# A transformer block on one Trainium2 core: the first FFN opened by token tile in a hand-written order, with the second half of x loaded behind four weight rows

## The chip, the cores and the metric

The kernel runs on one NeuronCore of a Trainium2 chip. The time is device microseconds of one execution. Three runs of the kernel before took 1849.17, 1852.2 and 1852.67 us; their median is 1852.2 us. The profiles come from single executions of their own; a profile's span runs from the first instruction to the last.

## The reference

One block of depth 1 over 256 tokens of width 2048, all in float32, with three parts in a row: a gated FFN (SwiGLU, inner width 5632), a mixer (differential attention beside a causal depthwise convolution), and a second FFN. Each part begins with an RMS norm, whose result is scaled and shifted by values that come from a conditioning vector `c`. The change concerns the first part alone:

```python
c_act = jax.nn.silu(c)
ada = jnp.einsum('bd,de->be', c_act, w_ada[l]) + b_ada[l]     # 9 x 2048 values
sh1, sc1, g1, ... = jnp.split(ada, N_MOD, axis=-1)
h = modulate(rms_norm(x, ffn1_norm[l]), sh1, sc1)             # h * (1 + sc1) + sh1
gu = jnp.einsum('bsd,df->bsf', h, w_gu); g, u = jnp.split(gu, 2, axis=-1)
x = x + FFN_RESIDUAL_WEIGHT * g1[:, None, :] * jnp.einsum('bsf,fd->bsd', jax.nn.silu(g) * u, w_down)
```

So before the first product with `w_gu` there must be: x and its root mean square for each token, the conditioning vector, and the scale and shift of the first 128 channels, which are dot products of `c_act` with rows of `w_ada`.

## The kernel before

**Tiles.** The 256 tokens are two tiles of 128 (t = 0, 1), the 2048 channels 16 tiles of 128 (k), the 11264 columns of `w_gu` 22 chunks of 512 (c). A weight row, here, is what one k brings to one chunk: 128 x 512 float32, 256 KB. Each float32 operand is split in two, a rounded part hi and a rest lo: ScalarE (ACT) casts hi, VectorE (DVE) subtracts to get lo. A product of one k, chunk and token tile is then three matmuls of 512 columns on TensorE (PE): ah x wh, ah x wl, al x wh (`mm3`, lines 316 to 318). A weight row so takes six matmuls for both token tiles, one split on ACT and one on DVE.

**Ada rows.** The modulation is computed on DVE. A row of 128 outputs is a 1 MB transfer and one multiply-and-sum over 2048 columns (`ada`, lines 181 and 182) against `c_bc`, the activated vector spread over all partitions by 16 PE transposes at the very start. Rows come in pairs, scale and shift of one k. The first two are brought and summed in halves (`first_modulation`, line 239), so that k = 0 is ready soon. `ada_next` counts the rows that have been traced, from 2 on.

**Opening.** h of a k can only be formed when its two ada rows are in. So the first chunks are not computed over a whole quarter of the channels (4 k), but over as many k as are ready: `EXT` gives the number for each chunk (1 for the first eight, 2 for four, 3 for three, then 4). `LOADS` says which chunks come in one transfer. Chunks with one k come through `w_first`, the others through `w_tile`. Their sums are kept in SBUF as `parts`. What is left of the quarter is made up later: the chunks in `AGAIN` are opened once more for their remaining k, and the result is added to the part by two DVE additions (line 538); the chunks in `EARLY` get their remaining k together with the next quarters in one accumulation.

**Order before.** x is loaded in two transfers right behind the constants. Both tiles' squares are summed, both are normed and transposed (`begin_both`, line 399 and 401), then `first_modulation` runs with the first weight row between its third and its fourth half, and `tile` (lines 387 to 389) forms hi and lo of h for both token tiles at once. In the loop at line 501 a chunk is loaded and split `AHEAD` = 3 steps before its products, ada rows follow the loads by `FIRST_ADA` and then by `DUE` (pairs of weight rows and ada rows that are due by then, with a straight line between), and `stage_a` makes the products of a chunk for both token tiles and copies them to the part (line 469).

**What sets the order.** The framework schedules the instructions of every engine ahead of time by its own cost figures; each engine then runs its own list strictly in order. `issue_after` adds an edge that puts instructions of an engine behind a given one on that engine; it is used for the transfers, all of which are on SP's queue. Buffers: 28 blocks of 4 KB per partition (`blk`), 4 raw buffers of 8 KB (shared by ada rows and full weight tiles), 4 hi and 4 lo buffers of two weight rows each, 6 accumulators in PSUM (`acc`) and 2 for transposes (`tp`).

Of the kernel before, what the change touches and what calls it, by code (L numbers as in the profile page):

```python
# [16 lines left out]
F32 = mybir.dt.float32  # L17
F32R = mybir.dt.float32r
# [9 lines left out]
NT = 2  # L28
# [9 lines left out]
DVE_COLS = 2  # L38
SOONER = 150
AHEAD = 3  # L40
EXT = (1,) * 8 + (2,) * 4 + (3,) * 3
LOADS = [(0,), (1,), (2, 3), (4, 5), (6, 7)] + [(c,) for c in range(8, NCH)]
FIRST_ADA = (0, 0, 1, 1, 1, 1, 1, 0, 1, 1, 1, 1)
AGAIN = [4, 5, 6]
EARLY = [[3, 8, 9], [4, 5, 6], [7, 10, 11], [12, 13, 14]]
EARLY_3 = [13, 14]

DUE = ((19, 8), (55, 16), (107, 24), (150, 32))


TAPS = (6, 8, 7, 6, 6, 6, 8, 6, 6, 6)
# [24 lines left out]
def block_kernel(ctx: ExitStack, tc: tile.TileContext, x_in, pos_in, w_ada, small, w_gu1, w_dn1,  # L76
# [41 lines left out]
    for t in range(NT):  # L118
        nc.sync.dma_start(out=xall[:, t, :], in_=x_in[t * P:(t + 1) * P, :])
# [75 lines left out]

    def ada_due(rows):

        r0, j0 = 0, 2
        for r, j in DUE:
# [26 lines left out]
            mods[base, k] = (G, a[:, j % 8 + 1:j % 8 + 2])  # L226
        return mods[base, k]

    def first_modulation(between):

        ada_cols[0] = const.tile([P, 8], F32, name="ada0")
        p0 = _COLS["bada"][0]
        a = sm([P, 4], "adah")
        for i in range(2):
            for h in range(2):
                between(2 * i + h)
                wa = blk([P, 1024])
                hs = slice(1024 * h, 1024 * h + 1024)
                nc.sync.dma_start(out=wa, in_=w_ada[i, :, hs])
                nc.vector.tensor_tensor_reduce(out=wa, in0=wa, in1=c_bc[:, hs], scale=1.0, scalar=0.0, op0=ALU.mult,  # L240
                                               op1=ALU.add, accum_out=a[:, 2 * i + h:2 * i + h + 1])
            nc.vector.scalar_tensor_tensor(out=ada_cols[0][:, i:i + 1], in0=a[:, 2 * i:2 * i + 1],
                                           scalar=cst[:, p0 + i:p0 + i + 1], in1=a[:, 2 * i + 1:2 * i + 2],
                                           op0=ALU.add, op1=ALU.add)
            if i == 0:
                nc.vector.scalar_tensor_tensor(out=scales[:, 0:1], in0=ada_cols[0][:, 0:1], scalar=1.0,
                                               in1=col("n1")[:, 0:1], op0=ALU.add, op1=ALU.mult)
        mods[0, 0] = (scales[:, 0:1], ada_cols[0][:, 1:2])
# [50 lines left out]
                views[k0 + h + j] = (hi[:, j, :], lo[:, j, :])  # L299
        return lambda j: views[j]  # L300

    def w_first(cs):
# [4 lines left out]
        hi = whp.tile([P, 2, 512], F32R, tag="whi", name=nm("whi"))  # L307
        lo = wlp.tile([P, 2, 512], F32R, tag="wlo", name=nm("wlo"))
        nc.scalar.copy(out=hi[:, :n, :], in_=raw[:, :n, :])
        nc.vector.tensor_sub(out=lo[:, :n, :], in0=raw[:, :n, :], in1=hi[:, :n, :].bitcast(F32))  # L310
        return [lambda j, i=i: (hi[:, i, :], lo[:, i, :]) for i in range(n)]

    def mm3(acc, a, w, start, stop):
        ah, al = a
        wh, wl = w
        nc.tensor.matmul(acc, ah, wh, start=start, stop=False)  # L316
        nc.tensor.matmul(acc, ah, wl, start=False, stop=False)  # L317
        return nc.tensor.matmul(acc, al, wh, start=False, stop=stop)  # L318

# [26 lines left out]
    class Norm:  # L346
# [41 lines left out]
            nc.vector.tensor_scalar(out=hf, in0=src, scalar1=G, scalar2=SH, op0=ALU.mult, op1=ALU.add)  # L388
            self.last = nc.vector.tensor_sub(out=self.hl[k // 4][:, k % 4, ts], in0=hf, in1=hi.bitcast(F32))  # L389

        def begin_both(self):
# [3 lines left out]
            for t in range(NT):  # L395
                self.done.add((0, t))
                self.rstd(t)
                xn = tmp([P, 512])
                nc.scalar.activation(out=xn, in_=x[0][:, t, :], func=AF.Identity, scale=self.r[t])
                for j in range(4):  # L400
                    nc.tensor.transpose(tps[j // 2][:, j % 2, t * P:(t + 1) * P], xn[:, j * P:(j + 1) * P], ident)
            return [tps[j // 2][:, j % 2, :] for j in range(4)]
# [39 lines left out]
    def ffn(st, w_gu, w_dn, gate_base, ada_a, ada_b, nxt, again, early, early_3):  # L442
# [36 lines left out]
        ext = [4] * NCH  # L479
        if not st.done:  # L480

            raws, begun = st.begin_both(), [0]
            ws = {}

            def load(i):
                cs = LOADS[i]
                if ext[cs[0]] == 1:
                    ws.update(zip(cs, w_first(cs)))
                else:
                    ws[cs[0]] = w_tile(w_gu[cs[0], 0], False, (0, ext[cs[0]]), ext[cs[0]] < 4)  # L490
# [3 lines left out]
            def begin_ready():
                while begun[0] < 4 and base + 2 * begun[0] + 2 <= ada_next[0]:
                    st.tile(raws[begun[0]], tmp([P, S]), (begun[0], slice(0, S)))
                    begun[0] += 1

            first_modulation(lambda n: load(0) if n == 3 else None)
            begin_ready()  # L500
            for i in range(len(LOADS) + AHEAD):
                if i < len(LOADS):
                    if i:
                        load(i)
                    with tc.issue_after(w_dma[0].ins):
                        if i < len(FIRST_ADA):
                            ada_until(ada_next[0] + FIRST_ADA[i])
                            rows[0] += ext[LOADS[i][0]] * len(LOADS[i])
                        else:
                            ada_a_share(ext[LOADS[i][0]])  # L510
# [677 lines left out]
```

## Time and profile before

| what | value |
| --- | --- |
| median of three runs | 1852.2 us |
| the profiled execution | 1848.81 us |
| its span | 1847.0 us |
| PE busy | 1820.2 us, 99% of the span |
| DVE busy | 1442.0 us, 78% |
| ACT busy | 911.9 us, 49% |
| mean granted TensorE clock | 0.996 |
| first matmul on a weight row | 17.66 us |

PE, DVE, ACT and POOL are the compute engines, SP the queue that issues the transfers. In a listing by time, a row gives the start and the length in us, engine, line, operation, output<-input and a count of merged instructions, then in brackets the idle time of the engine before it and what ended it. In a list of groups, the columns are count, busy us, mean ns of one, and the idle time before them with its releasers. In a table of windows the columns are the stretch, its length, busy time and number of instructions of PE, of its weight loads, of DVE, ACT and POOL, then the granted PE clock, the share of the DMA engines in use and GB/s. Matmuls are pipelined: the start of one to the start of the next is the time that it takes, not the length shown.

### The profile page before, as it was taken

What the parts mean: (1) busy time and instruction counts of PE and PEld (TensorE: products, weight loads), DVE (VectorE), ACT (ScalarE), POOL (GpSimd) and SP (SyncE); (2) the same over time, 40 slices, a digit from 0 to 9 for tenths busy, and PEclk for the clock granted to TensorE, in tenths of its full rate; (3) what the DMA queues carried; (4) which work ended last, traced back from release to release, by engine and by line L of the source; (5) the groups of instructions that cost most, each with busy time, mean ns of one, the idle gap of its engine ahead of it and who ended that gap; (6) DMA issues with size and microseconds to landing.
All of it is one profiled execution on the core that took longest, in us unless ns stands there. A gap on an engine that the chain in (4) does not pass through costs nothing.

```text
span 1847.0 us, 21889 instructions
## 1 busy us (share of the span) xinstructions
PE 1820.2 (99%) x8247; PEld 1501.6 (81%) x8247; DVE 1442.0 (78%) x1922; ACT 911.9 (49%) x1378; POOL 26.5 (1%) x29
## 2 busy tenths in 40 slices
PE   6999999999999999999999999999999999999999
PEld 5788888888888887878888888888888888888887
DVE  7789969998888777899999668878877765544443
ACT  6553444444444433554777655664444444433332
POOL 0000000000000000000110000000000000000000
PEclk8999999999999999999999999999999999999999
DMA  9888968888899898765544458888777755565552
GB/s 381 348 316 307 342 254 316 333 308 338 323 346 350 335 357 329 284 228 205 182 160 138 172 216 306 333 328 318 280 279 273 276 191 194 183 211 211 200 210 80
DMA packets 72729, 495.91 MB, mean 268 GB/s; under 512 B 8192, under 2 KB 8624, under 8 KB 15152
## 3 DMA queue, kind: packets, MB, share of 16 engines
q1 hardware_dynamic: 72624, 494.53, 72.1%
q8 instruction: 64, 1.05, 0.2%
q14 instruction: 41, 0.34, 0.1%
HBM read 492.37 MB, written 2.12 MB: 268 GB/s over the span
## 4 chain that ended last, share of the span: by engine, by line
PE 93%; DVE 3%; ACT 1%; DMA 1%; issue 1%; POOL 0%; SPq 0%; POOLq 0%; DVEq 0%; ACTq 0%
PE acc L317 30%; PE acc L318 30%; PE acc L316 30%; DVE blk L772 1%; PE tp L589 1%; DVE wlo L297 1%; DMA blk<-in_w_gu_dram 1%; PE acc L864 1%; PE tp L378 1%; DMA blk<-in_w_ada_dram 1%; ACT whi L295 0%; PE acc L903 0%; DVE raw L182 0%; ACT blk L469 0%; PE tp L813 0%
## 5 line engine op out<-in xcount | busy, mean ns | idle before, releaser
L295 ACT CAST whi<-raw 128x1024 fp32r<-128x1024 f32 (+1 forms) x605 | 628.4, 1046 | 737.5 <-PE acc L318 613.6
L297 DVE TENSOR_TENSOR wlo<-raw,whi 128x1024 fp32r<-128x1024 f32 (+1 forms) x605 | 725.7, 1212 | 318.3 <-ACT whi L295 316.9
L316 PE MATMUL acc<-whi,blk 128*128 128x512 f32 x2448 | 957.0, 393 | 5.8 <-ACT blk L387 2.2
L317 PE MATMUL acc<-wlo,blk 128*128 128x512 f32 x2448 | 956.7, 391 | 4.6 <-DVE wlo L297 4.6
L318 PE MATMUL acc<-whi,blk 128*128 128x512 f32 x2448 | 956.1, 391 | 0.1
L316 PEld LDWEIGHTS acc<-whi,blk 128*128 128x128 f32 x2448 | 460.5, 188 | 102.0 <-ACT whi L295 2.8
L317 PEld LDWEIGHTS acc<-wlo,blk 128*128 128x128 f32 x2448 | 460.6, 188 | 101.1 <-DVE wlo L297 8.0
L318 PEld LDWEIGHTS acc<-whi,blk 128*128 128x128 f32 x2448 | 460.2, 188 | 97.1 <-DVE blk L389 0.9
L182 DVE CUSTOM_DVE_ANT_0 raw<-raw,c_bc 128x2048 f32<-128x2048 f32 x142 | 324.4, 2285 | 5.3 <-DMA raw<-in_w_ada_dram 4.8
L772 DVE SCALAR_TENSOR_TENSOR blk<-blk,cst,blk 128x255 f32<-128x255 f32 (+17 forms) x240 | 97.5, 463 | 0.5 <-ACT blk L770 0.5
L469 ACT COPY blk<-acc 128x512 f32<-128x512 f32 x88 | 49.8, 591 | 60.6 <-PE acc L318 58.8
L581 DVE TENSOR_TENSOR blk<-acc,blk 128x512 f32<-128x512 f32 x88 | 56.9, 683 | 0.3
L318 PE MATMUL acc<-blk,blk 128*128 128x512 f32 x112 | 43.7, 392 | 0.0
L316 PE MATMUL acc<-blk,blk 128*128 128x512 f32 x112 | 43.7, 393 | 0.0
L317 PE MATMUL acc<-blk,blk 128*128 128x512 f32 x112 | 43.7, 390 | 0.0
L297 DVE TENSOR_TENSOR blk<-raw,blk 128x1024 fp32r<-128x1024 f32 x28 | 33.7, 1220 | 1.8 <-ACT blk L295 1.8
L583 DVE TENSOR_TENSOR blk<-blk 128x256 f32<-128x256 f32 x88 | 33.4, 418 | 0.7 <-ACT blk L582 0.7
L582 ACT ACTIVATE blk<-blk 128x256 f32<-128x256 f32 x88 | 32.2, 411 | 0.8 <-DVE blk L581 0.8
L295 ACT CAST blk<-raw 128x1024 fp32r<-128x1024 f32 x28 | 28.8, 1049 | 6.6 <-DMA raw<-in_w_dn_dram 5.3
L335 DVE TENSOR_TENSOR blk<-tp,blk 128x512 fp32r<-128x512 f32 x44 | 30.0, 684 | 2.3 <-ACT blk L334 2.3
L344 ACT ACTIVATE tmp<-xall 128x512 f32<-128x512 f32 x22 | 13.8, 631 | 31.2 <-DVE xall L642 17.8
L334 ACT CAST blk<-tp 128x512 fp32r<-128x512 f32 x44 | 25.3, 580 | 2.4 <-PE tp L589 2.4
(149 smaller groups left out, 662.8 us busy)
## 6 DMA issues: line engine op xcount, KB each, us to landing
raw<-in_w_gu_dram SPq DMA_DIRECT2D x161, 1024.0 KB, 5.2
raw<-in_w_ada_dram SPq DMA_DIRECT2D x142, 1024.0 KB, 5.9
raw<-in_w_dn_dram SPq DMA_DIRECT2D x88, 1024.0 KB, 4.8
raw<-in_w_in_dram SPq DMA_DIRECT2D x40, 1024.0 KB, 4.8
raw<-in_w_out_dram SPq DMA_DIRECT2D x16, 1024.0 KB, 4.8
raw<-in_w_gu_dram SPq DMA_DIRECT2D x8, 768.0 KB, 5.2
blk<-in_w_gu_dram SPq DMA_DIRECT2D x10, 512.0 KB, 14.1
blk<-gate_line SPq DMA_DIRECT2D x6, 512.0 KB, 5.6
```

What stands on the lines that cost most here:

```text
L182: nc.vector.tensor_tensor_reduce(out=raw, in0=raw, in1=c_bc, scale=1.0, scalar=0.0, op0=ALU.mult, op1=ALU.add, accum_out=ada_cols[g][:, j ...
L295: nc.scalar.copy(out=hi[:, :m, :], in_=rw)
L297: nc.vector.tensor_sub(out=lo[:, :m, :], in0=rw, in1=hi[:, :m, :].bitcast(F32))
L316: nc.tensor.matmul(acc, ah, wh, start=start, stop=False)
L317: nc.tensor.matmul(acc, ah, wl, start=False, stop=False)
L318: return nc.tensor.matmul(acc, al, wh, start=False, stop=stop)
L335: nc.vector.tensor_sub(out=lo, in0=tp, in1=hi.bitcast(F32))
L469: last_part[0] = nc.scalar.copy(out=parts[c][:, t, :], in_=accs[t])
L581: nc.vector.tensor_add(out=p[:, t, :], in0=accs[t], in1=p[:, t, :])
L582: nc.scalar.activation(out=p[:, t, :256], in_=p[:, t, :256], func=AF.Silu)
L583: nc.vector.tensor_mul(out=p[:, t, 256:], in0=p[:, t, :256], in1=p[:, t, 256:])
L772: nc.vector.scalar_tensor_tensor(out=y[:, d:], in0=u, scalar=w, in1=y[:, d:], op0=ALU.mult, op1=ALU.add)
```

## The change

The opening is traced by token tile.

- x of tile 0 is loaded as before; x of tile 1 is loaded behind the transfers of loads 0 to 2 (weight rows of chunks 0 to 3, `X_BEHIND`).
- Tile 0 alone is squared, normed and transposed, and then comes `first_modulation`, with no weight row between its halves.
- Loads 0 to 4 (chunks 0 to 7, one k each) are all issued at once; the hi and lo of loads 3 and 4 lie in blocks instead of the shared buffers. The splitting is now a function that is called later.
- A block under `manual_schedule` fixes the order of ACT, DVE and PE as written: splits, h of tile 0, its products with chunks 0 to 3, squares of tile 1, further splits and products, norm and transposes of tile 1, its h, ada rows 2 and 3, the products of chunks 6 and 7, then tile 1's products with all eight chunks, the load and split of chunks 8 and 9, and h of k = 1.
- In that block, tile 0's products of chunks 1 to 7 take al x wh before ah x wl.
- Ten chunks have one k, five have two, three have three; chunks 8 and 9 are one load. Seven chunks are opened again instead of three, and `DUE` has new pairs.
- In the loop that follows, DVE's part of a load and the ada rows are put behind the last h on DVE.

```diff
-EXT = (1,) * 8 + (2,) * 4 + (3,) * 3
-LOADS = [(0,), (1,), (2, 3), (4, 5), (6, 7)] + [(c,) for c in range(8, NCH)]
-FIRST_ADA = (0, 0, 1, 1, 1, 1, 1, 0, 1, 1, 1, 1)
-AGAIN = [4, 5, 6]
+EXT = (1,) * 10 + (2,) * 5 + (3,) * 3
+LOADS = [(0,), (1,), (2, 3), (4, 5), (6, 7), (8, 9)] + [(c,) for c in range(10, NCH)]
+BY_TILE = 5
+X_BEHIND = 2
+AGAIN = [4, 5, 6, 7, 15, 16, 17]
...
-DUE = ((19, 8), (55, 16), (107, 24), (150, 32))
+DUE = ((8, 4), (17, 6), (26, 8), (60, 16), (109, 24), (153, 32))
...
+        hi = blk([P, 2, 512], F32R) if held else whp.tile([P, 2, 512], F32R, tag="whi", name=nm("whi"))
+        lo = blk([P, 2, 512], F32R) if held else wlp.tile([P, 2, 512], F32R, tag="wlo", name=nm("wlo"))
+
+        def split():
+            nc.scalar.copy(out=hi[:, :n, :], in_=raw[:, :n, :])
+            nc.vector.tensor_sub(out=lo[:, :n, :], in0=raw[:, :n, :], in1=hi[:, :n, :].bitcast(F32))
...
+        if lo_last:
+            nc.tensor.matmul(acc, al, wh, start=False, stop=False)
+            return nc.tensor.matmul(acc, ah, wl, start=False, stop=stop)
...
+        def begin_sums(self, t):
+            self.done.add((0, t))
+            for n in range(4):
+                square_sum(n, t, self.ss, n % 2 == 1)
+            self.rstd(t)
+
+        def begin_norm(self, t):
+            self.xn = tmp([P, 512])
+            nc.scalar.activation(out=self.xn, in_=x[0][:, t, :], func=AF.Identity, scale=self.r[t])
+
+        def begin_transposes(self, t):
+            for j in range(4):
+                nc.tensor.transpose(self.raws[j][:, t * P:(t + 1) * P], self.xn[:, j * P:(j + 1) * P], ident)
...
+            st.begin_first()
+            st.begin_sums(0)
+            st.begin_norm(0)
+            st.begin_transposes(0)
+            first_modulation()
+            begun[0] = 1
+            split = []
+            for i in range(BY_TILE):
+                split.append(load(i))
+                if i == X_BEHIND:
+                    with tc.issue_after(w_dma[0].ins):
+                        w_dma[0] = load_x(1)
+                rows[0] += len(LOADS[i])
+            last_load = w_dma[0]
+
+            def first(t):
+                st.tile(st.raws[0][:, t * P:(t + 1) * P], tmp([P, P]), (0, slice(t * P, (t + 1) * P)))
+
+            def products(i, t):
+                for c in LOADS[i]:
+                    acc = acc_tile()
+                    mm3(acc, act(0, t), ws[c](0), True, True, i > 0 and t == 0)
+                    if parts[c] is None:
+                        parts[c] = blk([P, NT, 512])
+                    last_part[0] = nc.scalar.copy(out=parts[c][:, t, :], in_=acc)
+
+            with tc.manual_schedule(engines={mybir.EngineType.Activation, mybir.EngineType.DVE, mybir.EngineType.PE}):
+                split[0]()
+                first(0)
+                split[1]()
+                split[2]()
+                products(0, 0)
+                products(1, 0)
+                st.begin_sums(1)
+                split[3]()
+                products(2, 0)
+                st.begin_norm(1)
+                split[4]()
+                products(3, 0)
+                st.begin_transposes(1)
+                first(1)
+                with tc.issue_after(last_load.ins):
+                    ada_due(rows[0])
+                products(4, 0)
+                for i in range(BY_TILE):
+                    products(i, 1)
+                load(BY_TILE)
+                begin_ready()
+            for i in range(BY_TILE, len(LOADS) + AHEAD):
                 if i < len(LOADS):
-                    if i:
-                        load(i)
-                    with tc.issue_after(w_dma[0].ins):
...
+                    if i > BY_TILE:
+                        with tc.issue_after(st.last.ins):
+                            load(i)
+                    with tc.issue_after(w_dma[0].ins), tc.issue_after(st.last.ins):
+                        ada_a_share(ext[LOADS[i][0]] * len(LOADS[i]))
                         begin_ready()
-                if i >= AHEAD:
+                if i >= BY_TILE + AHEAD:
...
         for g in again:
+            n = 4 - ext[g]
...
-            ada_a_share(3)
+            ada_a_share(n)
```

More of the change, by code (lines that the diff above doesn't have):

```diff
@@ L117, in block_kernel, with load_x @@
     nc.sync.dma_start(out=cst[:, :first_cols], in_=small[:, :first_cols])
-    for t in range(NT):
-        nc.sync.dma_start(out=xall[:, t, :], in_=x_in[t * P:(t + 1) * P, :])
+    def load_x(t):
+        return nc.sync.dma_start(out=xall[:, t, :], in_=x_in[t * P:(t + 1) * P, :])
+    load_x(0)
     def col(name):
@@ L196, in ada_due @@
     def ada_due(rows):
-        r0, j0 = 0, 2
-        for r, j in DUE:
+        r0, j0 = DUE[0]
+        for r, j in DUE[1:]:
             if rows <= r:
@@ L227, in modulation, with first_modulation @@
         return mods[base, k]
-    def first_modulation(between):
+    def first_modulation():
         ada_cols[0] = const.tile([P, 8], F32, name="ada0")
@@ L235, in first_modulation @@
             for h in range(2):
-                between(2 * i + h)
                 wa = blk([P, 1024])
@@ L300, in w_tile, with w_first @@
         return lambda j: views[j]
-    def w_first(cs):
+    def w_first(cs, held):
         n = len(cs)
@@ L306, in w_first, with mm3 @@
         w_dma[0] = nc.sync.dma_start(out=raw[:, :n, :], in_=w_gu1[cs[0]:cs[0] + n, 0].rearrange("c p n -> p c n")[:, :, :512])
[L307 to L313, printed above, removed]
+        hi = blk([P, 2, 512], F32R) if held else whp.tile([P, 2, 512], F32R, tag="whi", name=nm("whi"))
[3 more added lines that the diff above has]
+            nc.vector.tensor_sub(out=lo[:, :n, :], in0=raw[:, :n, :], in1=hi[:, :n, :].bitcast(F32))
+        return [lambda j, i=i: (hi[:, i, :], lo[:, i, :]) for i in range(n)], split
+    def mm3(acc, a, w, start, stop, lo_last=False):
         ah, al = a
@@ L389, in tile, with begin_first @@
             self.last = nc.vector.tensor_sub(out=self.hl[k // 4][:, k % 4, ts], in0=hf, in1=hi.bitcast(F32))
-        def begin_both(self):
+        def begin_first(self):
             self.hh[0], self.hl[0] = blk([P, 4, S], F32R), blk([P, 4, S], F32R)
             tps = [tp_tile((P, 2, S)) for _ in range(2)]
[L395 to L402, printed above, removed]
+            self.raws = [tps[j // 2][:, j % 2, :] for j in range(4)]
+        def begin_sums(self, t):
[9 more added lines that the diff above has]
+                nc.tensor.transpose(self.raws[j][:, t * P:(t + 1) * P], self.xn[:, j * P:(j + 1) * P], ident)
         def piece(self, kb, t, fine=False):
@@ L480, in ffn @@
         if not st.done:
-            raws, begun = st.begin_both(), [0]
+            begun = [0]
             ws = {}
@@ L487, in load, with begin_ready @@
                 if ext[cs[0]] == 1:
-                    ws.update(zip(cs, w_first(cs)))
+                    views, split = w_first(cs, X_BEHIND < i < BY_TILE)
+                    ws.update(zip(cs, views))
+                    if i < BY_TILE:
+                        return split
+                    split()
                 else:
                     ws[cs[0]] = w_tile(w_gu[cs[0], 0], False, (0, ext[cs[0]]), ext[cs[0]] < 4)
+            def begin_ready():
+                while begun[0] < 4 and base + 2 * begun[0] + 2 <= ada_next[0]:
+                    st.tile(st.raws[begun[0]], tmp([P, S]), (begun[0], slice(0, S)))
+                    begun[0] += 1
@@ L492, in ffn @@
             for c in range(NCH):
                 ext[c] = EXT[c] if c < len(EXT) else 4
[L494 to L501, printed above, removed]
-                if i < len(LOADS):
-                    if i:
-                        load(i)
-                    with tc.issue_after(w_dma[0].ins):
[L506 to L510, printed above, removed]
+            st.begin_first()
@@ L746, in block_kernel @@
     norm2 = Norm(96, "n2", sm([P, NT, 4], "ss"))
-    for t in range(NT):
-        for n in range(4):
-            square_sum(n, t, norm1.ss, t == 0 and n % 2 == 1)
     ffn(norm1, w_gu1, w_dn1, 32, (0.78, 32), (0.78, 104), norm_m, AGAIN, EARLY, EARLY_3)
```

## The prediction

> **What bounds the kernel now.** I read the page first, then the windows of the span, then PE in order of time through the opening.
>
> ```profile
> span 1847.0 us, 21889 instructions
> ...
> PE 1820.2 (99%) x8247; PEld 1501.6 (81%) x8247; DVE 1442.0 (78%) x1922; ACT 911.9 (49%) x1378; POOL 26.5 (1%) x29
> ```
>
> ```profile
> 40.00:50.00 10.00, 9.47 (x42) 7.49 (x42) 9.93 (x13) 6.87 (x12) 0.00 (x0) 1.00 1.03 412
> ...
> 150.00:200.00 50.00, 50.00 (x225) 41.38 (x224) 46.40 (x57) 22.93 (x29) 0.00 (x0) 1.00 0.86 330
> ```
>
> PE sets the time: 50 of 50 us in the later window. In the opening it does not, while DVE (9.93 of 10) and the DMA (share 1.03) are full. The diff leaves the number of products as it is, so the end can move only by PE time lost in the opening, and by losses that are new later.
>
> ```profile
> 17.66 0.80 PE L316 MATMUL acc<-whi,blk 128*128 128x512 f32 x1 [2.18 <-ACT blk L387]
> ...
> 19.30 0.63 PE L316 MATMUL acc<-whi,blk 128*128 128x512 f32 x1
> ...
> 21.86 0.63 PE L318 MATMUL acc<-whi,blk 128*128 128x512 f32 x1
> ...
> 28.29 0.50 PE L316 MATMUL acc<-whi,blk 128*128 128x512 f32 x1 [0.66 <-ACT blk L469]
> ...
> 36.35 0.50 PE L316 MATMUL acc<-whi,blk 128*128 128x512 f32 x1 [0.54 <-ACT blk L469]
> ...
> 58.55 0.39 PE L318 MATMUL acc<-whi,blk 128*128 128x512 f32 x1
> 60.56 0.73 PE L316 MATMUL acc<-whi,blk 128*128 128x512 f32 x2 [1.62 <-ACT whi L295]
> 61.82 0.50 PE L317 MATMUL acc<-wlo,blk 128*128 128x512 f32 x1 [0.53 <-DVE wlo L297]
> ...
> 64.22 0.39 PE L316 MATMUL acc<-whi,blk 128*128 128x512 f32 x1
> ...
> 72.38 0.39 PE L316 MATMUL acc<-whi,blk 128*128 128x512 f32 x1
> ```
>
> ```profile
> L317 PE MATMUL acc<-wlo,blk 128*128 128x512 f32 x51 | 21.3, 418 | 1.1 <-DVE wlo L297 1.1
> L316 PE MATMUL acc<-whi,blk 128*128 128x512 f32 x52 | 20.9, 427 | 5.5 <-ACT blk L387 2.2 <-ACT whi L295 2.0 <-ACT blk L469 1.2
> L318 PE MATMUL acc<-whi,blk 128*128 128x512 f32 x50 | 20.6, 413 | 0.0
> ```
>
> **The yardstick.** From 64.22 to 72.38 there are 36 products, so one takes 8.16 / 36 = 0.2267 us when nothing waits; cold, from 19.30 to 21.86, six take 0.427 each. The second fence groups the first 62 us: 153 products, the last starting at 61.82. So 152 x 0.2267 = 34.5 us of work was done by then and the loss is 61.82 - 34.46 = **27.4 us**. I work out the same figure for the new opening. The profiled execution took 1848.81 us, its span and 1.8 around it; the median of the runs is 3.4 above it, so my difference is worked out on the one and added to the other.
>
> **The start.** x of tile 1 no longer stands ahead of the ada halves, nor row 0 ahead of the fourth half. The landing lines below are those of x, of the halves and of the first weight rows; then SP and DVE in order of time.
>
> ```profile
> DMA to landing us min/median/max: 4.9/5.9/6.9
> ...
> DMA to landing us min/median/max: 8.4/9.5/10.7
> ...
> DMA to landing us min/median/max: 9.9/11.4/12.9
> ```
>
> ```profile
> 1.17 0.89 SPq L119 DMA_DIRECT2D xall<-in_x_dram  x2
> ...
> 4.27 0.45 SPq L239 DMA_DIRECT2D blk<-in_w_ada_dram  x1
> ```
>
> ```profile
> 8.15 0.15 DVE L142 TENSOR_SCALAR rstd<-rstd 128x1 f32<-128x1 f32 x1
> 10.53 1.23 DVE L240 CUSTOM_DVE_ANT_0 blk<-blk,c_bc 128x1024 f32<-128x1024 f32 x1 [2.23 <-DMA blk<-in_w_ada_dram]
> ...
> 16.73 0.22 DVE L242 SCALAR_TENSOR_TENSOR ada<-adah,cst 128x1 f32<-128x1 f32 x1
> ```
>
> x lands at 6.1 and 8.5, so its second tile takes 2.4 us of the queue. The fourth half landed at 4.3 + 10.7 = 15.0. A row of 256 KB at 412 GB/s is 0.6. Without both the fourth half lands near 11.9, row 0 at 12.6, rows 2 and 3 near 15, x of tile 1 near 17.4, rows 4 to 7 by 20.3. SP issues all of them well ahead. DVE can then take the halves back to back from 8.3: 4 x 1.25 and some 0.6 of small operations end at 14.0, where now it is 16.95. The first product comes at 14.5 instead of 17.66: 3.1 us, if nothing came behind it.
>
> **ACT in the written order.** From there on one ACT program order carries everything.
>
> ```profile
> L469 ACT COPY blk<-acc 128x512 f32<-128x512 f32 x30 | 15.9, 599 | 4.7 <-PE acc L318 4.5
> ...
> L344 ACT ACTIVATE tmp<-xall 128x512 f32<-128x512 f32 x6 | 3.7, 630 | 1.1 <-DMA xall<-in_x_dram 1.1
> ...
> L309 ACT CAST whi<-blk 128x1024 fp32r<-128x1024 f32 x3 | 3.1, 1048 | 2.6 <-DMA blk<-in_w_gu_dram 2.6
> ...
> L388 DVE TENSOR_SCALAR tmp<-tp,scales,ada 128x256 f32<-128x256 f32 x4 | 2.2, 539 | 0.7 <-ACT blk L387 0.7
> ...
> L143 POOL TENSOR_TENSOR rstd<-rstd,half 128x1 f32<-128x1 f32 x2 | 2.0, 1009 | 10.7 <-DVE rstd L142 10.7
> L399 ACT ACTIVATE tmp<-xall,rstd 128x512 f32<-128x512 f32 x2 | 1.4, 719 | 1.7 <-POOL rstd L143 1.7
> ```
>
> Successive ACT operations overlap by about 0.1 us (15.9 us over 30 copies is 0.53 each), so I step by the durations less 0.1. From 14.05: hi of tile 0 and the casts of row 1 and of rows 2, 3 to 15.9; the copies of chunks 0 and 1 trail their cold products and end at 18.1; two squares of tile 1 to 19.35; cast of rows 4, 5 to 20.3; two copies to 21.3; the normed tile, behind DVE's sum and POOL's power, to 22.2; cast of rows 6, 7 to 23.1; two copies to 24.1; hi of tile 1 to 24.55. DVE stays inside this: lo of rows 6, 7 at 24.45, lo of h of tile 1 at 25.35. The 24 products of tile 1 then run from 25.4 to 30.85. Taking al before lo of the weights on tile 0 hides part of a DVE split; I give it nothing, since ACT is what is late there, and up to 0.6 (half a 1.22 us split) if DVE is. The held hi and lo buffers cost nothing: with 2 of h, 4 halves, 5 raw, 4 held and 8 parts, 23 of the 28 blocks are taken at most. Ada rows 2 and 3, 2.3 us each on DVE behind h of tile 1, lie under the 24 products.
>
> **The gap behind tile 1.** The cast of rows 8, 9 is traced behind the last copy of tile 1, on an engine held to that order. The present trace has the pattern:
>
> ```profile
> 58.30 1.26 ACT L469 COPY blk<-acc 128x512 f32<-128x512 f32 x2 [3.13 <-PE acc L318]
> 59.46 2.94 ACT L295 CAST whi<-raw 128x1024 fp32r<-128x1024 f32 x3
> ```
>
> There the last product starts at 58.55, its copy and a cast follow, the next product is at 60.56 and the one on lo at 61.82. From a last start at 30.6 the same chain gives: copy 31.05, cast 31.55, product 32.6, steady from 33.85. By then 49 products are done: loss 33.85 - 11.11 = 22.7. I add 0.4 for h of k = 1, which comes behind that split on DVE (0.54 and a subtraction) and holds chunk 10, and 0.6 for the openings of k = 2 and 3, where the present trace waits 0.54 and 0.66 behind ACT. Loss 23.7, so the opening gains **3.6 us**; without the gap the loss is 30.85 - 48 x 0.2267 + 0.6 = 20.6 and the gain 6.8.
>
> **DMA.** Up to row 28 the queue must bring 0.15 + 2 of x + 2 of halves + 6 of ada rows + 7.25 of weights, 17.4 MiB. At 412 GB/s from 3 us on that is 47 us, and PE asks for the last of it near 58.7: hidden, with 11 us to spare. What is late next is DVE.
>
> **The price later.** Four more chunks are reopened, each with two additions, and at row 26 ada stands at 8, where it now stands at 11 by row 25. The rows are the groups of 62 to 230 us.
>
> ```profile
> L297 DVE TENSOR_TENSOR wlo<-raw,whi 128x1024 fp32r<-128x1024 f32 x57 | 68.0, 1221 | 16.6 <-ACT whi L295 16.3
> ...
> L182 DVE CUSTOM_DVE_ANT_0 raw<-raw,c_bc 128x2048 f32<-128x2048 f32 x21 | 48.0, 2285 | 0.0
> ...
> L538 DVE TENSOR_TENSOR blk<-acc,blk 128x512 f32<-128x512 f32 x30 | 19.9, 687 | 2.8 <-PE acc L318 2.7
> ...
> L297 DVE TENSOR_TENSOR wlo<-raw,whi 128x512 fp32r<-128x512 f32 x11 | 7.5, 686 | 1.9 <-ACT whi L295 1.7
> ...
> L378 PE MATMUL tp<-cst,tmp 128*128 128x128 f32 x16 | 2.2, 272 | 0.0
> ```
>
> From row 45 to row 69 PE needs 24 x 6 x 0.2267 = 32.6 us. DVE needs, after: splits 7 x (1.22 + 0.69) + 3 x 0.69 = 15.4; additions 14 x 0.687 = 9.6; five ada rows with their small parts, 12.2; the first pieces of the next k, estimated at 3.0; in all 40.2. Before: 15.0 + 4.1 + 12.2 + 3.0 = 34.3. The debt is 7.6 us where it was 1.7. Against it stand: rows 29 to 45, where DVE needs 16 x 0.61 + 4 x 2.45 = 19.6 of PE's 21.8, so 2.2; the lead out of the opening, 3.4 (adding up DVE's work from 33.85 its last split there ends near 59.4, PE's products on it near 62.8); and PE's transposes, near 1.9. That is 7.5 against 7.6: covered, with nothing over. The bounds are 0 and 7.6; I take 1.4, near the lower, since the window of 150 to 200 us runs DVE at 46.4 of 50 without a wait of PE.
>
> **Sum.** 3.6 - 1.4 = 2.2 us gained: 1846.6 for the profiled execution, **1850.0** beside the median. About 0.2%, 3.7 us, is what a measurement of this kernel can tell from no change, so the forecast is no change.
>
> **Rivals.** *No gap at chunk 8.* If the cast of rows 8, 9 gets done ahead of the last copies, the opening gains 6.8, and DVE's debt takes 2.0 of it, since PE is further ahead: 4.8, so 1847.4. For it: the rows land by 27 and DVE is free from 30.1. Against it: the traced order.
>
> *The clock stays low.*
>
> ```profile
> 22.00:23.00 1.00, 1.00 (x4) 0.81 (x3) 0.74 (x2) 1.00 (x2) 0.00 (x0) 0.50 0.97 397
> 23.00:24.00 1.00, 1.00 (x4) 0.76 (x4) 0.94 (x1) 1.00 (x3) 0.00 (x0) 0.73 1.02 397
> ```
>
> The granted clock goes from 0.50 to full at about 23.5, after 5.9 us of products without a break since 17.66. The new opening has products from 14.5 to 19.7, 5.2 us, and then breaks of about 0.7 and 0.4. If that is too short, chunks 6 and 7, the transposes and the first of tile 1's products are cold: some 10 x 0.2 us, so 2.0 lost, a gain of 0.2 and 1852.0. [...]
>
> *DVE's debt isn't covered.* Place: chunks 15 to 17 reopened with one row each (1.36 us of PE against 0.69 + 1.37 of DVE and an ada share) and the first pieces right behind. If DVE comes out of the opening without a lead and gains none up to row 45, the whole 7.6 is paid: 3.6 - 7.6, slower by 4.0, 1856.2. It decides from a lead of 4.0 us at row 45 downwards. For it: DVE at 9.93 of 10 even now. Against: its waiting for casts (16.3 us in the groups of 62 to 230 us), which shows room.
>
> **How the numbers follow.** Forecast 0.34, no gap 0.27, cold clock 0.20, debt 0.19. Faster by over 0.2%: the no-gap case and a twentieth from the forecast's own spread, 0.32. Slower: the debt case, less the part of it where some lead remains, 0.16. Within: 0.52. The range goes from the no-gap case with a smaller debt, 1845.0, to the debt in full, 1856.0; the forecast's own is 1848 to 1852.
>
> **What would show it.** The first product near 14.5 and tile 1's first near 25.4; a PE wait of 1.6 us on the cast of rows 8, 9 near 32 and a shorter one on its lo; no DMA wait of a cast after 30; DVE near full from 35 to 120 us and PE waits on lo or acc buffers at the reopened chunks, 1.4 us in all. The step that is wrong is the gap's if PE runs through at 31, the ACT order's if tile 1 starts later than 26.5, and the debt's if the waits from 60 to 120 us sum to 0 or to over 4.

## The result and the profile after

The changed kernel takes 1856.97 us (median of 6 runs, 1855.99 to 1858.51); the kernel before took 1850.72 us beside it. The ratio is 1.0034, 95% interval 1.0024 to 1.0045: 0.34% slower. The profiled execution took 1855.99 us. Its page begins:

```profile
span 1854.2 us, 21923 instructions
...
PE 1822.1 (98%) x8247; PEld 1501.6 (81%) x8247; DVE 1447.9 (78%) x1937; ACT 912.6 (49%) x1376; POOL 26.5 (1%) x29
```

The span grew by 7.2 us and PE was busy for 1.9 us more, so most of the growth is time in which PE waited. The opening, by PE in order of time (in the changed kernel L322 to L327 are the matmuls of `mm3`, L314 casts the first chunks, and L298 and L300 split the others on ACT and DVE):

```profile
14.50 0.79 PE L322 MATMUL acc<-whi,blk 128*128 128x512 f32 x1 [1.27 <-ACT blk L396]
...
20.66 0.50 PE L322 MATMUL acc<-blk,blk 128*128 128x512 f32 x1 [1.58 <-ACT blk L314]
...
25.66 0.40 PE L322 MATMUL acc<-whi,blk 128*128 128x512 f32 x1
...
30.89 0.39 PE L327 MATMUL acc<-blk,blk 128*128 128x512 f32 x1
32.90 1.67 PE L322 MATMUL acc<-whi,blk 128*128 128x512 f32 x6 [1.62 <-ACT whi L314]
```

First product at 14.50, tile 1 from 25.66, the last of its products at 30.89, and then the gap on the cast of chunks 8 and 9: 1.62 us. Where the rest went shows when the prediction's yardstick is taken at several times: time, less 0.2267 us for each product of 512 columns so far, less 0.11 us for each transpose of a piece. It is PE's loss up to then.

| loss of PE up to (us) | 48 | 66 | 84 | 105 | 125 | 160 | 300 |
| --- | --- | --- | --- | --- | --- | --- | --- |
| before | 24.2 | 27.5 | 27.3 | 27.5 | 27.4 | 27.5 | 27.6 |
| after | 22.8 | 24.3 | 24.4 | 25.7 | 34.4 | 34.4 | 34.7 |

(Each entry moves by about 0.1 with the product at which it is cut, and by more where PE stands in a wait at that time.) The opening gained about 3.0 us, and 10.0 us were lost between 84 and 125 us. After that the two run alike. The net, 7.0, is close to the 7.2 by which the span grew. In windows, the changed kernel first, then the one before:

```profile
96.00:100.00 4.00, 4.00 (x19) 3.31 (x18) 4.00 (x5) 1.02 (x2) 0.00 (x0) 1.00 0.38 139
104.00:108.00 4.00, 2.92 (x13) 2.12 (x12) 3.78 (x7) 0.62 (x1) 0.00 (x0) 1.00 0.90 271
108.00:112.00 4.00, 1.35 (x6) 0.77 (x5) 4.00 (x6) 0.00 (x0) 0.00 (x0) 1.00 0.92 320
112.00:116.00 4.00, 2.14 (x4) 1.33 (x5) 3.19 (x8) 3.00 (x4) 0.00 (x0) 0.64 1.10 423
116.00:120.00 4.00, 4.00 (x11) 3.05 (x11) 3.74 (x10) 2.91 (x8) 0.00 (x0) 0.51 0.92 360
```

```profile
104.00:108.00 4.00, 4.00 (x21) 3.29 (x20) 4.00 (x5) 1.53 (x2) 0.00 (x0) 1.00 0.57 201
...
112.00:116.00 4.00, 4.00 (x19) 3.30 (x19) 4.00 (x7) 3.64 (x5) 0.00 (x0) 1.00 0.22 90
```

Before, PE is full here, although the DMA share goes as low as 0.22, so a low share alone cost PE nothing there. After, the DMA share falls to 0.38, DVE is busy for 19.75 of the 20 us from 92 to 112, PE drops to 1.35 of 4, and then the granted clock goes to 0.51 and products come 0.43 us apart instead of 0.23 until 119.5. By engine in order of time (ACT, then PE, DVE and SP), and what SP waited for between 85 and 115 us (us in total, times, longest); L287 issues weight tiles and L185 ada rows:

```profile
99.29 0.63 ACT L298 CAST whi<-raw 128x512 fp32r<-128x512 f32 x1 [2.89 <-DMA raw<-in_w_gu_dram]
101.33 0.62 ACT L298 CAST whi<-raw 128x512 fp32r<-128x512 f32 x1 [1.41 <-DMA raw<-in_w_gu_dram]
105.21 0.62 ACT L298 CAST whi<-raw 128x512 fp32r<-128x512 f32 x1 [3.26 <-DMA raw<-in_w_gu_dram]
112.72 1.57 ACT L298 CAST whi<-raw 128x1024 fp32r<-128x1024 f32 x2 [6.90 <-DMA raw<-in_w_gu_dram]
```

```profile
105.88 0.73 PE L322 MATMUL acc<-whi,blk 128*128 128x512 f32 x2 [1.08 <-ACT whi L298]
113.82 1.22 PE L322 MATMUL acc<-whi,blk 128*128 128x512 f32 x2 [4.47 <-ACT whi L298]
```

```profile
105.01 1.89 DVE L300 TENSOR_TENSOR wlo<-raw,whi 128x512 fp32r<-128x512 f32 x3
107.11 3.68 DVE L602 TENSOR_TENSOR blk<-acc,blk 128x512 f32<-128x512 f32 x6 [0.22 <-PE acc L327]
```

```profile
94.77 7.26 SPq L287 DMA_DIRECT2D raw<-in_w_gu_dram  x3
...
103.92 0.33 SPq L185 DMA_DIRECT2D raw<-in_w_ada_dram  x1
105.72 1.98 SPq L287 DMA_DIRECT2D raw<-in_w_gu_dram  x3
```

```profile
SPq L185 <- DVE tmp L442: 6.3, 1, 6.3
SPq L185 <- DVE ada L186: 5.8, 2, 5.3
SPq L287 <- DVE ada L186: 5.4, 2, 3.6
SPq L287 <- DVE wlo L300: 4.8, 3, 2.6
```

The casts of 128x512 at 99.29, 101.33 and 105.21 are those of the reopened chunks 15, 16 and 17, one row each. Each row lies in a raw buffer until DVE has split it, and DVE, busy with additions and ada rows in its order, splits all three only from 105.01 on. SP's queue stands for buffers on the way, the next three tiles are issued only from 105.72 to 107.70, and the cast of the chunk behind comes at 112.72.

### The profile page after: what moved, and what is told of

The parts are those of the page before. It is cut to its first block, busy times and chain, and to the rows that moved or that the text cites. A ratio compares the mean times of both kernels' runs of the same rounds, so it can differ in the third digit from the quotient of the medians.

```text
span 1854.2 us, 21923 instructions
## 1 busy us (share of the span) xinstructions
PE 1822.1 (98%) x8247; PEld 1501.6 (81%) x8247; DVE 1447.9 (78%) x1937; ACT 912.6 (49%) x1376; POOL 26.5 (1%) x29
## 4 chain that ended last, share of the span: by engine, by line
PE 92%; DVE 3%; DMA 2%; ACT 1%; issue 1%; POOL 0%; SPq 0%; POOLq 0%; DVEq 0%; ACTq 0%
PE acc L326 30%; PE acc L327 30%; PE acc L322 30%; DMA blk<-in_w_gu_dram 1%; PE tp L654 1%; DVE blk L834 1%; DVE wlo L300 1%; PE acc L926 1%; PE tp L387 0%; DMA blk<-in_w_ada_dram 0%; ACT whi L298 0%; DMA raw<-in_w_gu_dram 0%; DVE raw L186 0%; PE tp L875 0%; DVE blk L602 0%
## 5 line engine op out<-in xcount | busy, mean ns | idle before, releaser
L298 ACT CAST whi<-raw 128x1024 fp32r<-128x1024 f32 (+1 forms) x604 | 626.5, 1045 | 752.0 <-PE acc L327 622.9
L300 DVE TENSOR_TENSOR wlo<-raw,whi 128x1024 fp32r<-128x1024 f32 (+1 forms) x604 | 723.8, 1212 | 307.7 <-ACT whi L298 306.4
L322 PE MATMUL acc<-whi,blk 128*128 128x512 f32 x2440 | 952.2, 393 | 8.7 <-ACT whi L298 5.6
L327 PE MATMUL acc<-whi,blk 128*128 128x512 f32 x2437 | 951.1, 390 | 0.1
L322 PEld LDWEIGHTS acc<-whi,blk 128*128 128x128 f32 x2440 | 458.8, 188 | 103.9 <-ACT whi L298 6.6
L327 PEld LDWEIGHTS acc<-whi,blk 128*128 128x128 f32 x2437 | 458.1, 188 | 96.7 <-DVE blk L398 0.6
L485 ACT COPY blk<-acc 128x512 f32<-128x512 f32 x72 | 41.6, 589 | 57.4 <-PE acc L327 55.0
L646 DVE TENSOR_TENSOR blk<-acc,blk 128x512 f32<-128x512 f32 x88 | 56.9, 684 | 0.2
L322 PE MATMUL acc<-blk,blk 128*128 128x512 f32 x120 | 47.0, 394 | 1.6 <-ACT blk L314 1.6
L327 PE MATMUL acc<-blk,blk 128*128 128x512 f32 x116 | 45.2, 391 | 0.0
L326 PE MATMUL acc<-blk,blk 128*128 128x512 f32 x116 | 45.2, 390 | 0.0
L300 DVE TENSOR_TENSOR blk<-raw,blk 128x1024 fp32r<-128x1024 f32 x28 | 33.8, 1223 | 1.8 <-ACT blk L298 1.8
L602 DVE TENSOR_TENSOR blk<-acc,blk 128x512 f32<-128x512 f32 x44 | 28.7, 686 | 7.5 <-PE acc L327 7.5
L648 DVE TENSOR_TENSOR blk<-blk 128x256 f32<-128x256 f32 x88 | 33.5, 420 | 0.7 <-ACT blk L647 0.7
L298 ACT CAST blk<-raw 128x1024 fp32r<-128x1024 f32 x28 | 28.8, 1049 | 6.8 <-DMA raw<-in_w_dn_dram 5.3
L322 PEld LDWEIGHTS acc<-blk,blk 128*128 128x128 f32 x120 | 22.5, 188 | 6.4 <-ACT blk L314 2.0
```

Source lines behind the costliest of these rows:

```text
L298: nc.scalar.copy(out=hi[:, :m, :], in_=rw)
L300: nc.vector.tensor_sub(out=lo[:, :m, :], in0=rw, in1=hi[:, :m, :].bitcast(F32))
L485: last_part[0] = nc.scalar.copy(out=parts[c][:, t, :], in_=accs[t])
L646: nc.vector.tensor_add(out=p[:, t, :], in0=accs[t], in1=p[:, t, :])
L648: nc.vector.tensor_mul(out=p[:, t, 256:], in0=p[:, t, :256], in1=p[:, t, 256:])
```

## The experiments

Times are medians, the ratio that to the kernel before measured beside it. "Loss" is the yardstick above in the profiled execution.

### Old sizes in the new opening

```diff
-EXT = (1,) * 10 + (2,) * 5 + (3,) * 3
+EXT = (1,) * 8 + (2,) * 4 + (3,) * 3
-AGAIN = [4, 5, 6, 7, 15, 16, 17]
+AGAIN = [4, 5, 6]
-DUE = ((8, 4), (17, 6), (26, 8), (60, 16), (109, 24), (153, 32))
+DUE = ((8, 4), (13, 6), (19, 8), (55, 16), (107, 24), (150, 32))
```

> Keeps the opening by token tile up to tile 1's products and sets EXT, LOADS from chunk 8 on, AGAIN and the due times from row 19 on back to those of before (three chunks reopened, none with a single row). Theory: the 10 us that PE loses from 84 to 120 us in the changed kernel come from the reopened chunks 15 to 17 and what stands around them; then the loss there goes to under 1 us and the opening's gain of 3 us is kept: about 1847 to 1849 beside 1850.7 of before. Rival (the opening itself shifts the engines so that the later stretch suffers): a loss of 5 us or more stays between 80 and 125 us and the time stays at 1854 or above.

1853.42 us, 1.0014 (1.0005 to 1.0022). The loss up to 84 us is 29.1, more than before the change; from there to 125 it is 2.3. PE in order of time:

```profile
46.33 0.50 PE L326 MATMUL acc<-wlo,blk 128*128 128x512 f32 x1 [2.34 <-DVE wlo L300]
```

So the burst does belong to the sizes, the reopened chunks with them. But the opening's gain was not kept, which neither the theory nor its rival had: the order by tile with the old sizes is worse than the old opening. DVE does ada rows from 37.47, 40.82 and 46.19 us on and splits between them, PE waits for it, and from 47.39 to about 50.7 us products come 0.43 us apart instead of 0.23, which is part of the 29.1.

### The three rows apart, without additions, in other buffers, with later additions

```diff
e2_inter:    +AGAIN = [15, 4, 16, 5, 17, 6, 7]
e3_no_add:   +            if g < 15:
                 add_part(g, accs)
e4_blk_raw:  +            w = w_tile(w_gu[g, 0], False, (ext[g], 4), n == 1)
e8_late_add: -            add_part(g, accs)
             +            owed.append((g, accs))
             +            if len(owed) > 1:
             +                add_part(*owed.pop(0))
             ...
```

e14_blk_no_add is e3 and e4 together. e3 and e14 leave the last row of chunks 15 to 17 out of the result.

> The changed kernel with the seven reopened chunks in the order 15, 4, 16, 5, 17, 6, 7, so that no two single-row chunks stand next to each other; work, transfers and additions are the same in number. Theory (a burst: three single-row tiles hold three of four raw buffers for 1.36 us of PE work each while DVE is late, and SP's queue stands): the loss from 84 to 120 us falls from 10 us to 4 or less, time about 1850 to 1852. Rival (DVE's whole work in that stretch is too much): the sum of DVE's work is the same, so 8 us or more remain, time 1855 or above.

> The changed kernel without the two DVE additions for each of chunks 15, 16 and 17 after they are reopened (their last row is left out of the result): 6 x 0.69 = 4.1 us less for DVE at that place; buffers and transfers as they are. Theory of raw buffers: the transfers behind still wait for buffers, 5 us or more of the 10 remain. Rival (DVE's work is the bound from 92 to 113 us): each us taken from DVE comes back as a us of PE, and the cold clock with it, so 4 us or less remain, time 1849 to 1852.

> The changed kernel with the raw rows of the reopened chunks 15 to 17 in blocks of 4 KB instead of the four raw buffers; DVE's work is unchanged. Theory of raw buffers: SP no longer stands at 95 to 102 us, the DMA does not fall idle, the cast at 112.7 comes 4 us or more sooner, and the loss falls from 10 to 4 us or less. Rival (DVE's work): DVE is as full as before, 8 us or more remain, only the waits get other names.

> The changed kernel with the two additions of a reopened chunk traced one chunk later. Taking away 4.1 us of additions alone and giving the single rows other buffers alone returned 0 and 2.4 of the 10 us. New theory: DVE, in program order, stands 3.2 us at the first reopened chunk's addition (87.4 to 90.7 us in those runs) while casts wait to be split; raw buffers then come free late, SP's queue stands behind them, and PE runs dry at 105 to 114. With the additions later that idle time goes and the loss from 84 to 125 us falls from 10 to 6 us or less. Rival (the order of DVE is not the trigger, three single-row tiles in a row are): 8 us or more remain.

> The changed kernel with the single raw rows in blocks and without the additions of chunks 15 to 17 (their last row is left out of the result). Theory of two limits in series: alone these returned 2.4 and 0 of the 10 us, together 5 or more, loss between 84 and 125 us at 5 or less. Rival: they add up, 7 us or more remain.

| | time (us) | ratio, interval | loss at 84 | loss at 160 | lost between |
| --- | --- | --- | --- | --- | --- |
| changed kernel | 1856.97 | 1.0034 (1.0024 to 1.0045) | 24.4 | 34.4 | 10.0 |
| e2_inter | 1853.04 | 1.0012 (1.0003 to 1.0021) | 24.8 | 30.6 | 5.8 |
| e3_no_add | 1858.59 | 1.0039 (1.0026 to 1.0053) | 25.7 | 36.0 | 10.3 |
| e4_blk_raw | 1855.81 | 1.0023 (1.0014 to 1.0032) | 25.3 | 32.9 | 7.6 |
| e8_late_add | 1855.9 | 1.0028 (1.0018 to 1.0037) | 24.8 | 33.5 | 8.7 |
| e14_blk_no_add | 1852.18 (one run) | none | 25.3 | 30.1 | 4.8 |

Without the additions nothing came back (e3): DVE then stood idle for an ada row that had not landed, and ACT for weights.

```profile
112.43 2.29 DVE L186 CUSTOM_DVE_ANT_0 raw<-raw,c_bc 128x2048 f32<-128x2048 f32 x1 [3.10 <-DMA raw<-in_w_ada_dram]
```

```profile
114.40 1.56 ACT L298 CAST whi<-raw 128x1024 fp32r<-128x1024 f32 x2 [5.18 <-DMA raw<-in_w_gu_dram]
```

So DVE's amount of work alone is not the bound in the changed kernel. With the rows in other buffers (e4) the transfers were early, and DVE was next: six additions and an ada row stood ahead of the following split. The loss, 7.6, is nearer to the rival's 8 than to the theory's 4. DVE and ACT of e4:

```profile
107.74 3.67 DVE L602 TENSOR_TENSOR blk<-acc,blk 128x512 f32<-128x512 f32 x6
111.33 2.27 DVE L186 CUSTOM_DVE_ANT_0 raw<-raw,c_bc 128x2048 f32<-128x2048 f32 x1
113.54 0.08 DVE L186 DVE_READ_ACCUMULATOR2_ANT ada<- 128x1 f32 x1
113.54 1.21 DVE L300 TENSOR_TENSOR wlo<-raw,whi 128x1024 fp32r<-128x1024 f32 x1
```

```profile
107.84 1.57 ACT L298 CAST whi<-raw 128x1024 fp32r<-128x1024 f32 x2 [3.72 <-DVE wlo L300]
```

Both taken away together left 4.8 of 10.0, in a single run, where one alone returned 2.4 and the other nothing: two limits in series, the raw buffers and DVE. Keeping the single rows apart, with no work taken out (e2), returned 4.2; the 5.8 that remain lie between what the theory (4 or less) and its rival (8 or more) had said. e8 was meant to take away DVE's wait at the first addition, and returned 1.3. But the wait is still in its profile, as long as in the changed kernel's (there at 89.25):

```profile
89.72 1.38 DVE L602 TENSOR_TENSOR blk<-acc,blk 128x512 f32<-128x512 f32 x2 [3.24 <-PE acc L327]
```

The additions were traced one chunk later, but the first ones stand at the same place in DVE's order; only the later ones came to lie between the splits. So whether that wait is the trigger is not tested by any run here.

### The parts of the opening

```diff
e5_gap:        for i in range(BY_TILE):
             +     if i == 3:
             +         load(BY_TILE)
                   products(i, 1)
             - load(BY_TILE)
e6_x_first:    load_x(0)
             + load_x(1)
e10_rows_only (the kernel before, with the sizes of the change):
             +FIRST_ADA = (0, 0, 1, 0, 1, 0, 0, 1, 0, 1, 0, 1)
             +AGAIN = [4, 5, 6, 7, 15, 16, 17]
             +DUE = ((26, 8), (60, 16), (109, 24), (153, 32))
             ...
```

> The changed kernel with the load and split of chunks 8 and 9 written two loads earlier in the fixed order (behind the copies of chunks 2 and 3 of tile 1). Theory: PE's wait of 1.6 us on that cast at 32.9 and the one on its lo go, and PE's loss at 84 us falls from 24.4 by 2 to 3 us; as the stretch of the reopened chunks is bound by other engines it gives part of it back, so the time falls by 0 to 3 us from 1857. Rival: the gap is filled by another wait at once (h of k = 1 late) and the loss at 84 us stays within 1 us.

> The changed kernel with x of tile 1 loaded right behind x of tile 0, as before the change; all else as changed. Theory: the first product moves from 14.5 to about 17 (2.4 us of queue), tile 1 is no longer waited for, and the loss at 84 us grows by 1 to 2.5 us. Rival: ACT's order hides it, the loss at 84 us stays within 0.7 us.

> The kernel before, with only the sizes of the change: EXT, LOADS, AGAIN, the due times, and a FIRST_ADA that brings ada rows at the changed kernel's rows; x, norm and products by both tiles at once as before. The run with the old sizes in the new opening lost 29.3 us by 84 us, more than the 27.4 of before. Theory: the gain of the opening comes from the sizes (fewer ada rows early), not from the order by tile: the loss at 84 us is 25 us or less here, and the reopened chunks lose 5 to 10 us, so 1853 to 1858. Rival: the order by tile brings it; then the loss at 84 us stays at 26.5 or above.

e5: 1854.09 us, 1.0015 (1.0007 to 1.0024); the gap is gone and the loss at 84 us is 22.6. That is 1.8 less than in the changed kernel's profile, and 2.7 less than in that of e4, where the products of the opening were slow for as long as in e5: al x wh on chunks 1 to 3 of tile 0 has a mean length of 550 ns in e4 and 551 in e5, and products were slow again from about 22 to 25.4 us in both (the granted clock of e4 reads 0.53, 0.50, 0.50 and 0.76 from 22 to 26). e6: 1859.43, 1.0044 (1.0030 to 1.0058); first product at 16.88, loss at 84 us 26.2, that is 1.8 above the changed kernel and 0.5 to 1.4 above runs with the same opening whose clock rose later or fell again (below), so what the place of x is worth is not settled between its theory and its rival. e10: 1853.51, 1.0008 (0.9999 to 1.0017), and it decides where the opening's gain comes from. Its PE:

```profile
17.70 0.80 PE L316 MATMUL acc<-whi,blk 128*128 128x512 f32 x1 [2.18 <-ACT blk L387]
...
33.74 0.51 PE L316 MATMUL acc<-whi,blk 128*128 128x512 f32 x1 [0.44 <-ACT blk L469]
...
110.50 0.73 PE L316 MATMUL acc<-whi,blk 128*128 128x512 f32 x2 [4.62 <-ACT whi L295]
```

It starts as late as ever, 17.70, and then has one wait of 0.44 us up to 84: loss there 20.8, against 27.3 before and 24.4 with the order by tile. The sizes (more chunks on the first k, three ada rows fewer by row 26) are worth some 6.5 us in the opening; the order by tile and x behind the rows, the gap at chunks 8 and 9 among it, take 3.6 of them away. The burst at the reopened chunks is the same here (20.8 to 30.1) with the old opening in front: it comes with the sizes.

### Mending the sizes

```diff
e12_early (on e10_rows_only; the old EARLY goes):
-AGAIN = [4, 5, 6, 7, 15, 16, 17]
+AGAIN = [4, 5, 6, 7]
+EARLY = [[3, 8, 9], [4, 5, 6], [7, 10, 11], [12, 13, 14], [15, 16, 17]]
e15_early_due (on e12_early):
+DUE = ((26, 8), (45, 14), (60, 16), (109, 24), (153, 32))
e16_early_late: e12_early with the additions of e8_late_add
e17_tile_fixed: the changed kernel with e5_gap and e12_early
e11_blk_late: e10_rows_only with e4_blk_raw and e8_late_add
e13_inter_blk_late: e11_blk_late with the order of e2_inter
```

> The kernel before with the sizes alone (e10_rows_only), with single raw rows in blocks and the additions traced one chunk later. Theory: the loss of the reopened chunks (9.5 us there from 84 to 115 us) is two limits one behind the other, raw buffers that each bring only one row, and DVE's program order (six additions and an ada row ahead of chunk 3's split); each alone returned under 2.5 us, both together return 5 us or more: loss at 160 us 25 us or less, about 1848. Rival (DVE's total work): 28 us or more.

> As e11_blk_late, with the reopened chunks in the order 15, 4, 16, 5, 17, 6, 7. Theory: the order spreads what is left; the loss at 160 us is 1 to 3 us under that of e11_blk_late. Rival: blocks and order do the same thing once, no difference.

> The kernel before with the sizes alone, but chunks 15, 16 and 17 are not reopened for one row: they form a fifth group of EARLY, where their row opens an accumulation of two more quarters' rows. Theory: without the burst of single rows ahead of the first pieces the loss between 84 and 125 us falls from 9.5 to 3 us or less and the opening's 20.8 is kept: about 1845 to 1848, faster than both kernels. Rival (four reopened chunks with the first pieces are already too much): 6 us or more remain there.

> e12_early (the kernel before with the sizes, chunks 15 to 17 in a fifth group of EARLY) with one more due point: 14 ada rows by row 45 instead of 12, so less ada work from row 45 to 60. Theory (what is left, 3.9 us, is DVE late at the reopened chunks with five ada rows among them): loss between 84 and 125 us 1 to 2.5 us, about 1847. Rival: the ada rows then crowd out splits from 66 to 84 us, loss moves there, total within 1 us of e12_early.

> e12_early with the additions of the reopened chunks traced one chunk later. Theory (DVE stands 3.2 us in program order at the first addition, before it is late): loss between 84 and 125 us 1 to 2.5 us instead of 3.9. Rival, as in the changed kernel where this alone returned about 1 us: 3 us or more remain.

> The changed kernel (opening by token tile) with both losses mended: rows 8 and 9 cast earlier (as e5_gap) and chunks 15 to 17 in a fifth group of EARLY (as e12_early). Theory: the order by tile itself is worth less than both tiles at once with the same sizes: loss near 22.5 at 84 us against 21.2 of e12_early, and the same 4 us behind, so about 1 to 2 us above e12_early: 1849 to 1851. Rival: with the gap closed the order by tile is as good or better: at or under e12_early.

| | time (us) | ratio, interval | loss at 84 | loss at 160 |
| --- | --- | --- | --- | --- |
| e11_blk_late | 1851.44 | 1.0006 (0.9997 to 1.0015) | 21.2 | 29.0 |
| e13_inter_blk_late | 1850.39 | 0.9999 (0.9990 to 1.0008) | 22.8 | 27.9 |
| e12_early | 1848.82 | 0.9990 (0.9981 to 0.9999) | 21.2 | 25.2 |
| e15_early_due | 1851.86 | 1.0002 (0.9993 to 1.0011) | 25.3 | 28.3 |
| e16_early_late | 1849.09 | 0.9990 (0.9981 to 0.9999) | 21.9 | 27.0 |
| e17_tile_fixed | 1849.14 | 0.9991 (0.9982 to 1.0000) | 22.6 | 26.3 |

e11 is a miss. On this opening, other buffers and spread additions together returned 1.5 of 9.3 us (21.2 to 29.0), where I had expected 5 or more; its rival, DVE's total work, is what came. PE's waits there are on DVE's splits, 4.9 us in all, and DVE is busy for 20 of the 20 us from 92 to 112. The order of e13 returned 1.1 more by 160 us (its 22.8 at 84 us is cut inside a wait; it is 21.3 at 66 us).

e12 keeps the opening and loses 4.0 us at the reopened chunks instead of 9.3. Its time is 0.1% under that of the kernel before, with an interval that only just leaves out no change, and it is faster than the changed kernel. Its waits left there, by PE:

```profile
88.70 0.50 PE L317 MATMUL acc<-wlo,blk 128*128 128x512 f32 x1 [0.58 <-DVE wlo L297]
...
103.56 0.50 PE L317 MATMUL acc<-wlo,blk 128*128 128x512 f32 x1 [2.31 <-DVE wlo L297]
```

These are waits on DVE, not on transfers. Neither ada rows moved earlier (e15: the loss moved ahead of 84 us, and the time is 3.0 us above e12's) nor additions traced later (e16) mended them. With both mends the order by tile (e17) is 1.1 us behind e12 by the yardstick and 0.3 us by the times, which cannot be told apart. What the last 4 us are stays open; DVE's wait of 3.2 us at the first addition is still there in e11, e12 and e16, so it has not been excluded.

## Why the prediction was wrong, point by point

The forecast was no change, 1850.0; the result is slower by 6.25 us (1856.97 less 1850.72), just above the range. The forecast stood beside 1852.2 for the kernel before; beside the 1850.72 of six runs the same 2.2 us of gain would be 1848.5.

- **Start and ACT order: right.** First product 14.5 forecast, 14.50 measured; tile 1 at 25.4, measured 25.66; last product 30.6 against 30.89.
- **The gap: right.** Product on rows 8, 9 at 32.6, measured 32.90; the no-gap rival did not occur. Closing it by hand (e5) returned 1.8 to 2.7 us at 84 us; the prediction had 3.2 (6.8 less 3.6).
- **Loss of the opening 23.7, gain 3.6: the number nearly right,** 24.4 and 3.0, **the reason not.** The new opening was followed step by step as it came; but the gain was put down to the early start, and e10, which starts at 17.70, gains 6.5. It came from the sizes, and the order by tile cost 3.6 of it; I counted the effect of fewer ada rows only as a thing hidden. Part of the closeness is luck with the clock, too (next point).
- **The clock rival: not in this profile, but in others.** Here the granted clock was full from about 17.5 us, 3.0 us after the first product, until 113 us. With the same opening products came at full speed only from 19.10 us on in e3 and from about 19.9 in e8. In e3 and e4 the clock fell to 0.50 again for 3.4 us, from 22.4 and 22.1 us on. In e2 and e14 the products on the lo of chunks 4 to 7 of tile 0 were slow too, with mean lengths of 551 and 538 ns; these are 573 and 553 in e3 and e4, and 448 and 446 here and in e8. In e2, e3, e4 and e14 the loss at 84 us was 0.4 to 1.3 us higher. The stretch was near the rival's (the transposes lie in it: the eight have a mean length of 426 ns in e3 and 353 here); its price, 2.0, was too high, and it had a late rise where there was a rise and a fall.

```profile
16.00:17.00 1.00, 1.00 (x4) 0.80 (x3) 0.39 (x1) 1.00 (x2) 0.00 (x0) 0.50 0.92 373
17.00:18.00 1.00, 1.00 (x4) 0.57 (x4) 0.83 (x1) 0.60 (x2) 0.00 (x0) 0.74 1.03 391
```

- **"The price later", 1.4 us: the step that failed.** It measured 10.0 us, outside the bounds of 0 and 7.6. I summed DVE's work against PE's from row 45 to 69, found the debt of 7.6 covered by 7.5 of slack and lead, and left the buffers out. What the runs show in its place is a feed that stops at the reopened single rows, with two limits in series. The first is turnover of buffers: a reopened single row holds a whole raw buffer and a place in SP's queue for 1.36 us of PE's work, ada rows hold others for none, and each comes free only when DVE, in program order, gets to it. The second is DVE itself. The same work in another order returned 4.2 us (e2), other buffers alone 2.4 (e4), 4.1 us less work alone nothing (e3), the two together 5.2 (e14), and without the single rows 4.0 were lost instead of 9.3 (e12 beside e10). How the rest divides between DVE's work, its order and its wait at the first addition is not shown. Against the lead of 3.4 us that I had counted stands that wait of 3.24 us, whose price no run shows. The rival on DVE's debt had the place and the sign; its price, 7.6, is near the 7.4 that stay without the clock (below), but its mechanism, work alone, is contradicted by e2 and e3, so the nearness is luck at least in part. The prediction's own sentence on DMA, hidden with 11 us to spare, was worked out up to row 28 only.
- **Then the clock was low as well.** Behind the 4.47 us wait the granted clock was 0.51, and products took 0.427 us instead of 0.227 from 113.8 to 119.5, some 13 products: 2.6 of the 10.0 us. I had weighed the clock at the start and not behind a later wait.

## What to carry to other kernels

Price a smaller tile not only by its work but by the buffer and the queue place that it holds: here three tiles of one row, in buffers for four, went with a DMA share of 0.38 and then a PE wait of 4.47 us. When a change mixes a new order with new sizes, run the sizes alone; here they gained 6.5 us in the opening and lost 9.3 behind it. Look for slow products behind a long PE wait in mid-kernel: here they cost 2.6 us on top of the 4.47, and they came behind the 4.62 us wait of e10 as well, though not behind one of 2.31 us in e12. And when an edit is meant to take a wait away, look in the new trace whether it has gone: in e8 it had not.

## What was not expected of the hardware

The clock's first rise did not come at a fixed point of the kernel, and in some profiles the clock fell again soon after it. In the changed kernel's profile it rose at about 17.5 us and stayed. In that of e3, whose opening is the same, products still took 0.43 us each up to 18.62 and 0.23 from 19.10 on (the granted clock reads 1.00 there from before the first product, which the products contradict), and it fell at about 22.4 us:

```profile
18.62 0.64 PE L325 MATMUL acc<-wlo,blk 128*128 128x512 f32 x1
19.10 0.39 PE L322 MATMUL acc<-whi,blk 128*128 128x512 f32 x1
19.33 0.40 PE L324 MATMUL acc<-whi,blk 128*128 128x512 f32 x1
```

```profile
22.00:23.00 1.00, 0.47 (x2) 0.34 (x2) 0.60 (x1) 0.94 (x2) 0.00 (x0) 0.69 0.98 385
24.00:25.00 1.00, 1.00 (x5) 0.70 (x5) 0.27 (x1) 1.00 (x2) 0.00 (x0) 0.50 0.97 395
```

With the same opening the loss up to 84 us was 24.4, 24.8, 24.8, 25.3, 25.3 and 25.7 in the profiles of the changed kernel, e2, e8, e4, e14 and e3; that spread of 1.3 us is as large as some of the effects studied. What makes the clock fall is not shown. In the changed kernel it fell at about 113.1 us, inside the wait of 4.47 us. In e10 the two products right behind the wait of 4.62 us, at 110.50, still came at full speed, and those from 112.35 to 114.48 came 0.43 us apart. In e1 products came 0.43 us apart from 47.39 us on, soon after a wait of 2.34 us, while in e12 they came 0.23 apart behind one of 2.31 us. The idle time ahead of it does not tell e3 from the changed kernel either: from 19 to 22 us PE was busy for 1.56 of the 3 us in e3, where the clock then fell, and for 0.89 in the changed kernel, where it stayed at 1.00.
